# Token-major products read their moving columns in groups of four, odd groups first

## The chip, the cores and the metric

The kernel runs on one core of one Trainium2 chip. The metric is device time in microseconds for one execution of the whole program. The kernel before takes 3138.79 us (median of 3 runs, 3138.43 to 3139.48).

## The reference

Two transformer-like blocks over 256 tokens with 2048 features each, in float32. The first has a joint input projection, stick-breaking attention and chunked attention with relative bias, two sigmoid gates, an output projection, a gated feed-forward part with 5632 hidden features, and a gated addition from a second input. The second has a state-space branch, a gated linear attention branch, differential attention, three gates, an output projection, and a feed-forward part with a three-tap convolution over the tokens and 5504 hidden features. Cut to what matters here, every large step is a product of activations with a weight matrix that is read once:

```python
proj = h @ w_in[i]
merged = (jax.nn.sigmoid(gate_sb) * (y_sb @ w_sb_out[i])
          + jax.nn.sigmoid(gate_ca) * (y_ca @ w_ca_out[i]))
x = x + merged @ w_mix_out[i]
h = rmsnorm(x, g_ffn[i])
g_ff, u_ff = jnp.split(h @ w_ffn_in[i], 2, axis=-1)
x = x + (jax.nn.silu(g_ff) * u_ff) @ w_ffn_out[i]
```

With 256 tokens and some 580 MB of weights, the products are the work.

## The kernel before

**Precision.** A float32 product is made of three products in the format `fp32r`. Each factor is split into a high part (a cast to `fp32r`) and a low part (the rest): high x high, high x low and low x high are summed in PSUM. The split of the activations is kept in slots of 128 x 4 x 512, in which each feature tile has 256 high and 256 low columns. The split of the weights is made on the way: a DMA on the SP queue (line 476) brings half a megabyte, 128 x 1024, into a raw buffer; ACT casts it into the high ring (line 485, `high`), DVE subtracts for the low ring (line 495, `low`). Both rings lie in one tile `w`: five places of 1024 elements for the high parts, four for the low parts.

**Two kinds of products.** A *layer-major* job (`WS`) has the weights as the stationary operand and the tokens as the moving one: line 545 streams 512 columns (high and low tokens) through a high weight tile, line 549 streams 256 through a low one. The result has features on the partitions. A *token-major* job (`AS`) has the tokens as the stationary operand, 128 at a time, and the weights as the moving one: 512 weight columns stream through the tokens. The result has tokens on the partitions and 512 features along them. `mm_as` issues these: for each of the two feature tiles of a half and each of two token groups `m` there are three products, line 583 (low tokens, high weights), line 584 (high tokens, low weights) and line 585 (high, high). The very first half of the program takes another order, lines 573, 575 and 576. Each matmul instruction of the program carries its own weight load (LDWEIGHTS), which TensorE runs beside the matmul ahead of it.

**Order.** `stream` goes over all jobs in the order of the program and issues, half by half, the cast four halves ahead, the subtraction three halves ahead, the products of the half, and then lets the other generators (evacuation, attention, scans, norms) take one step. There is no scheduler behind it: each engine runs what was issued, in that order.

**Places.** When the halves of a layer-major job lie at the end of a ring turn, their places are shifted by `WSH` = 4 elements, 16 bytes (`places`, `far`). Token-major halves are never shifted.

**Layout.** The weights are laid out on the host before the timed run. `_as` makes the token-major layout: for each 512 columns, blocks of 256 rows as 128 partitions x 2 x 512. All token-major weights go through `_as` and are read by `mm_as` alone.

Of the kernel before, what the change touches and what calls it, by code (L numbers as in the profile page):

```python
# [53 lines left out]

def _as(w):

    K, N = w.shape
    if K % 256:
        w = np.concatenate([w, np.zeros((256 - K % 256, N), w.dtype)], axis=0)
        K = w.shape[0]  # L60
    return np.ascontiguousarray(
        w.reshape(K // 256, 2, 128, N // 512, 512).transpose(3, 0, 2, 1, 4).reshape(-1, 128, 1024))
# [12 lines left out]
def layout(x, p, w_in, w_sb_out, w_ca_out, w_mix_out, rel_bias, g_mix, g_ffn, g_ple, g_final, w_ffn_in,  # L75
# [35 lines left out]

    w = w_in[0]
    a["w_vsb"], a["w_vca"] = _as(w[:, 2048:3072]), _as(w[:, 5120:6144])
    a["w_qksb"] = _ws(w[:, 0:1024], w[:, 1024:2048])
    a["w_qkca"] = _ws(w[:, 3072:4096], w[:, 4096:5120])
    a["w_gsb"], a["w_gca"] = _as(w[:, 6144:8192]), _as(w[:, 8192:10240])
    a["w_sbo"], a["w_cao"], a["w_mix"] = _as(w_sb_out[0]), _as(w_ca_out[0]), _as(w_mix_out[0])
    a["w_fin"] = _ws(w_ffn_in[0][:, :5632], w_ffn_in[0][:, 5632:])
    a["w_fout"] = _as(w_ffn_out[0])
# [68 lines left out]
class Build:  # L188
# [373 lines left out]
    def mm_as(self, acts, ks, wh, wl, acc, ms, first, end, low_last=False):  # L562

        nc = self.nc
        if low_last:
            for low in (False, True):
                for kk, k in enumerate(ks):
                    s = slice(kk * 512, kk * 512 + 512)
                    for m in ms:
                        x = acts.at(k)  # L570
                        xh, xl = x[:, m * 128:m * 128 + 128], x[:, 256 + m * 128:384 + m * 128]
                        if low:
                            nc.tensor.matmul(acc[:, m, :], lhsT=xh, rhs=wl[:, s], start=False, stop=False)
                        else:
                            nc.tensor.matmul(acc[:, m, :], lhsT=xl, rhs=wh[:, s], start=k == first, stop=False)
                            nc.tensor.matmul(acc[:, m, :], lhsT=xh, rhs=wh[:, s], start=False, stop=False)
            return
        for kk, k in enumerate(ks):
            x = acts.at(k)
            s = slice(kk * 512, kk * 512 + 512)  # L580
            for m in ms:
                xh, xl = x[:, m * 128:m * 128 + 128], x[:, 256 + m * 128:384 + m * 128]
                nc.tensor.matmul(acc[:, m, :], lhsT=xl, rhs=wh[:, s], start=k == first, stop=False)  # L583
                nc.tensor.matmul(acc[:, m, :], lhsT=xh, rhs=wl[:, s], start=False, stop=False)  # L584
                nc.tensor.matmul(acc[:, m, :], lhsT=xh, rhs=wh[:, s], start=False, stop=k == end)  # L585


    def as_job(self, w, n, acts, evac, k0=0, nk=None, before=None, kt=None):
# [1205 lines left out]
```

## Time and profile before

| | before |
|---|---|
| median of 3 runs | 3138.79 us |
| profiled execution, whole | 3139.36 us |
| its span, first to last instruction | 3137.6 us |
| mean granted TensorE clock | 0.999 |
| TensorE busy | 3119.9 us, 99% |
| weight loads busy | 2651.4 us, 85% |
| DVE busy | 1993.1 us, 64% |
| ACT busy | 1553.3 us, 50% |
| moved by DMA | 618.00 MB, mean 197 GB/s |

PE is TensorE's matmuls, PEld its weight loads, DVE the vector engine, ACT the scalar engine. A row of a group gives the line, the engine, the operation, output and inputs with their shapes, the number of instructions, then the busy time in us (overlaps counted once), the mean duration of one in ns, and the idle time ahead of them with what ended it. A matmul's duration holds its way through the array, and the next one starts before it ends; the ends are modelled. A timeline row gives the start in us from the first instruction and the duration in us.

### The profile page before, as it was taken

What the parts mean: (1) busy time and instruction counts of PE and PEld (TensorE: products, weight loads), DVE (VectorE), ACT (ScalarE), POOL (GpSimd) and SP (SyncE); (2) the same over time, 40 slices, a digit from 0 to 9 for tenths busy, and PEclk for the clock granted to TensorE, in tenths of its full rate; (3) what the DMA queues carried; (4) which work ended last, traced back from release to release, by engine and by line L of the source; (5) the groups of instructions that cost most, each with busy time, mean ns of one, the idle gap of its engine ahead of it and who ended that gap; (6) DMA issues with size and microseconds to landing.
All of it is one profiled execution on the core that took longest, in us unless ns stands there. A gap on an engine that the chain in (4) does not pass through costs nothing.

```text
span 3137.6 us, 45166 instructions
## 1 busy us (share of the span) xinstructions
PE 3119.9 (99%) x17629; PEld 2651.4 (85%) x17629; DVE 1993.1 (64%) x2593; ACT 1553.3 (50%) x2035; POOL 73.4 (2%) x158
## 2 busy tenths in 40 slices
PE   9999999999999999999999999999999999999998
PEld 7888888888888888888888888888888888888887
DVE  5656445557577677566655667945555766757766
ACT  6544444455444454456544454444445654545545
POOL 0000000000001000000000001000000000000000
PEclk9999999999999999999999999999999999999999
DMA  7554555555667766655654575655555555555554
GB/s 265 170 180 163 189 194 187 182 189 189 216 224 243 255 224 233 198 175 189 216 181 162 174 221 197 211 191 199 200 186 181 190 195 186 191 196 188 192 188 168
DMA packets 172645, 618.00 MB, mean 197 GB/s; under 512 B 23552, under 2 KB 23968, under 8 KB 169232
## 3 DMA queue, kind: packets, MB, share of 16 engines
q1 hardware_dynamic: 164992, 577.49, 55.4%
q0 software_dynamic: 7440, 37.64, 3.5%
q8 instruction: 138, 2.26, 0.3%
q14 instruction: 75, 0.61, 0.1%
HBM read 599.74 MB, written 14.25 MB: 196 GB/s over the span
## 4 chain that ended last, share of the span: by engine, by line
PE 99%; ACT 0%; DMA 0%; DVE 0%; DVEq 0%; issue 0%; SPq 0%; ACTq 0%
PE acc L545 29%; PE acc L583 17%; PE acc L584 17%; PE acc L585 17%; PE acc L549 15%; PE p L348 1%; PE p L1699 0%; PE p L1739 0%; PE p L1156 0%; PE p L930 0%; PE p L931 0%; PE p L932 0%; PE p L1152 0%; PE p L1742 0%; PE p L1133 0%; PE p L1733 0%
## 5 line engine op out<-in xcount | busy, mean ns | idle before, releaser
L495 DVE TENSOR_TENSOR w<-raw,w 128x1024 fp32r<-128x1024 f32 x1088 | 1320.2, 1220 | 644.2 <-PE acc L584 421.7
L485 ACT CAST w<-raw 128x1024 fp32r<-128x1024 f32 x1088 | 1138.4, 1049 | 1092.4 <-PE acc L585 637.3
L545 PE MATMUL acc<-s,w 128*128 128x512 f32 x3936 | 1369.5, 393 | 0.0
L549 PE MATMUL acc<-s,w 128*128 128x256 f32 x3936 | 1090.4, 282 | 0.0
L583 PE MATMUL acc<-w,s 128*128 128x512 f32 x2372 | 932.4, 393 | 0.8 <-DVE big L1376 0.8
L585 PE MATMUL acc<-w,s 128*128 128x512 f32 x2372 | 923.6, 389 | 0.0
L584 PE MATMUL acc<-w,s 128*128 128x512 f32 x2372 | 923.5, 389 | 0.0
L545 PEld LDWEIGHTS acc<-s,w 128*128 128x128 f32 x3936 | 733.4, 188 | 153.5
L549 PEld LDWEIGHTS acc<-s,w 128*128 128x128 f32 x3936 | 740.2, 188 | 10.4 <-issue 1.0
L583 PEld LDWEIGHTS acc<-w,s 128*128 128x128 f32 x2372 | 445.6, 188 | 93.8 <-issue 1.7
L585 PEld LDWEIGHTS acc<-w,s 128*128 128x128 f32 x2372 | 445.3, 188 | 93.5
L584 PEld LDWEIGHTS acc<-w,s 128*128 128x128 f32 x2372 | 445.7, 188 | 90.9 <-issue 0.5
L445 DVE TENSOR_TENSOR s<-acc,s 128x512 f32<-128x512 f32 (+1 forms) x120 | 82.7, 690 | 263.8 <-ACT s L444 263.7
L444 ACT COPY s<-acc 128x512 f32<-128x512 f32 (+1 forms) x120 | 70.1, 585 | 189.1 <-PE acc L545 186.9
L312 ACT ACTIVATE s<-s 128x256 f32<-128x256 f32 (+4 forms) x175 | 76.6, 443 | 105.1 <-DVE s L315 38.0
L315 DVE SCALAR_TENSOR_TENSOR s<-s,conv 128x256 f32<-128x256 f32 x172 | 79.4, 482 | 3.1
L447 DVE TENSOR_TENSOR s<-s,rb 128x512 f32<-128x512 f32 (+1 forms) x104 | 71.7, 689 | 3.5
L320 ACT CAST s<-s 128x256 fp32r<-128x256 f32 (+1 forms) x104 | 45.7, 443 | 30.1 <-DVE s L970 15.0
L1655 DVE TENSOR_TENSOR s<-s,s 128x1024 f32<-128x1024 f32 x48 | 58.5, 1220 | 0.0
L312 ACT ACTIVATE s<-s,conv 128x256 f32<-128x256 f32 x86 | 47.1, 595 | 22.0 <-DVE s L447 22.0
L321 DVE TENSOR_TENSOR s<-s,s 128x256 fp32r<-128x256 f32 (+1 forms) x104 | 47.6, 460 | 15.8 <-ACT s L320 15.8
L312 ACT ACTIVATE junk<-big 128x512 f32<-128x512 f32 x48 | 30.3, 632 | 50.7 <-DVE big L949 32.4
(265 smaller groups left out, 1007.7 us busy)
## 6 DMA issues: line engine op xcount, KB each, us to landing
raw<-in_w_fin SPq DMA_DIRECT2D x176, 512.0 KB, 4.3
raw<-in_w_up SPq DMA_DIRECT2D x172, 512.0 KB, 4.0
raw<-in_w_fout SPq DMA_DIRECT2D x88, 512.0 KB, 4.3
raw<-in_w_down SPq DMA_DIRECT2D x84, 512.0 KB, 4.2
raw<-in_w_qksb SPq DMA_DIRECT2D x32, 512.0 KB, 3.8
raw<-in_w_qkca SPq DMA_DIRECT2D x32, 512.0 KB, 3.5
raw<-in_w_gsb SPq DMA_DIRECT2D x32, 512.0 KB, 3.9
raw<-in_w_gca SPq DMA_DIRECT2D x32, 512.0 KB, 4.2
```

Source lines behind the costliest of these rows:

```text
L312: self.nc.scalar.activation(out, in_, func, scale=scale, **kw)
L315: self.nc.vector.scalar_tensor_tensor(out=out, in0=in0, scalar=scalar, in1=in1, op0=op0, op1=op1)
L444: nc.scalar.copy(out, acc[:, 0:n, 256:512])
L445: nc.vector.tensor_add(out, acc[:, 0:n, 0:256], out)
L447: nc.vector.tensor_mul(out, out, rb.tile[:, None, :].to_broadcast([128, n, 256]) if n > 1 else rb.tile[:, None, :])
L485: nc.scalar.copy(wh[:, :n], raws[i][:, :n])
L495: nc.vector.tensor_sub(wl[:, :n], r[:, :n], wh[:, :n].bitcast(F32))
L545: hi = lambda: nc.tensor.matmul(acc[:, f, :], lhsT=wh[:, s], rhs=x, start=k == first, stop=k == end)
L549: nc.tensor.matmul(acc[:, f, 256:512], lhsT=wl[:, s], rhs=x[:, 0:256], start=False, stop=False)
L583: nc.tensor.matmul(acc[:, m, :], lhsT=xl, rhs=wh[:, s], start=k == first, stop=False)
L584: nc.tensor.matmul(acc[:, m, :], lhsT=xh, rhs=wl[:, s], start=False, stop=False)
L585: nc.tensor.matmul(acc[:, m, :], lhsT=xh, rhs=wh[:, s], start=False, stop=k == end)
```

## The change

The columns of each 512-wide block of a token-major weight are permuted on the host. Taken in groups of four (16 bytes), the stored order is: group 0 of the first 256 columns, group 0 of the second 256, group 1 of the first, group 1 of the second, and so on. `mm_as` then reads the moving operand with a pattern of three levels: two passes, 64 groups each, four columns in each group. The first pass takes the first, third, fifth .. group, the second pass the others. The columns arrive at TensorE, and in PSUM, in their old order. The patterns of the stationary operand, of PSUM and of the weights' casts and subtractions stay as they are.

```diff
 def _as(w):
     K, N = w.shape
+    w = w.reshape(K, N // 512, 2, 64, 4).transpose(0, 1, 3, 2, 4).reshape(K, N)
     if K % 256:
...
     def mm_as(self, acts, ks, wh, wl, acc, ms, first, end, low_last=False):
         nc = self.nc
+        def cols(w, kk):
+            return w[:, kk * 512:kk * 512 + 512].rearrange("p (i h c) -> p h i c", h=2, c=4)
...
         for kk, k in enumerate(ks):
             x = acts.at(k)
-            s = slice(kk * 512, kk * 512 + 512)
             for m in ms:
                 xh, xl = x[:, m * 128:m * 128 + 128], x[:, 256 + m * 128:384 + m * 128]
-                nc.tensor.matmul(acc[:, m, :], lhsT=xl, rhs=wh[:, s], start=k == first, stop=False)
-                nc.tensor.matmul(acc[:, m, :], lhsT=xh, rhs=wl[:, s], start=False, stop=False)
-                nc.tensor.matmul(acc[:, m, :], lhsT=xh, rhs=wh[:, s], start=False, stop=k == end)
+                nc.tensor.matmul(acc[:, m, :], lhsT=xl, rhs=cols(wh, kk), start=k == first, stop=False)
+                nc.tensor.matmul(acc[:, m, :], lhsT=xh, rhs=cols(wl, kk), start=False, stop=False)
+                nc.tensor.matmul(acc[:, m, :], lhsT=xh, rhs=cols(wh, kk), start=False, stop=k == end)
```

The three products of the first half (`low_last`) are changed in the same way.

More of the change, by code (lines that the diff above doesn't have):

```diff
@@ L572, in mm_as @@
                         if low:
-                            nc.tensor.matmul(acc[:, m, :], lhsT=xh, rhs=wl[:, s], start=False, stop=False)
+                            nc.tensor.matmul(acc[:, m, :], lhsT=xh, rhs=cols(wl, kk), start=False, stop=False)
                         else:
-                            nc.tensor.matmul(acc[:, m, :], lhsT=xl, rhs=wh[:, s], start=k == first, stop=False)
-                            nc.tensor.matmul(acc[:, m, :], lhsT=xh, rhs=wh[:, s], start=False, stop=False)
+                            nc.tensor.matmul(acc[:, m, :], lhsT=xl, rhs=cols(wh, kk), start=k == first, stop=False)
+                            nc.tensor.matmul(acc[:, m, :], lhsT=xh, rhs=cols(wh, kk), start=False, stop=False)
             return
@@ L579, in mm_as @@
             x = acts.at(k)
-            s = slice(kk * 512, kk * 512 + 512)
             for m in ms:
                 xh, xl = x[:, m * 128:m * 128 + 128], x[:, 256 + m * 128:384 + m * 128]
-                nc.tensor.matmul(acc[:, m, :], lhsT=xl, rhs=wh[:, s], start=k == first, stop=False)
-                nc.tensor.matmul(acc[:, m, :], lhsT=xh, rhs=wl[:, s], start=False, stop=False)
-                nc.tensor.matmul(acc[:, m, :], lhsT=xh, rhs=wh[:, s], start=False, stop=k == end)
+                nc.tensor.matmul(acc[:, m, :], lhsT=xl, rhs=cols(wh, kk), start=k == first, stop=False)
+                nc.tensor.matmul(acc[:, m, :], lhsT=xh, rhs=cols(wl, kk), start=False, stop=False)
+                nc.tensor.matmul(acc[:, m, :], lhsT=xh, rhs=cols(wh, kk), start=False, stop=k == end)
     def as_job(self, w, n, acts, evac, k0=0, nk=None, before=None, kt=None):
```

## The prediction

> **What bounds the kernel now.** I read the profile page first (busy shares, the chain that ended last, the costliest groups), then the timeline of one long stretch of token-major products, then three places where the same product runs under other conditions. The page:
>
> ```profile
> span 3137.6 us, 45166 instructions
> ...
> PE 3119.9 (99%) x17629; PEld 2651.4 (85%) x17629; DVE 1993.1 (64%) x2593; ACT 1553.3 (50%) x2035; POOL 73.4 (2%) x158
> ...
> PEclk9999999999999999999999999999999999999999
> ...
> PE 99%; ACT 0%; DMA 0%; DVE 0%; DVEq 0%; issue 0%; SPq 0%; ACTq 0%
> PE acc L545 29%; PE acc L583 17%; PE acc L584 17%; PE acc L585 17%; PE acc L549 15%; PE p L348 1%; PE p L1699 0%; PE p L1739 0%; PE p L1156 0%; PE p L930 0%; PE p L931 0%; PE p L932 0%; PE p L1152 0%; PE p L1742 0%; PE p L1133 0%; PE p L1733 0%
> ...
> L545 PE MATMUL acc<-s,w 128*128 128x512 f32 x3936 | 1369.5, 393 | 0.0
> L549 PE MATMUL acc<-s,w 128*128 128x256 f32 x3936 | 1090.4, 282 | 0.0
> L583 PE MATMUL acc<-w,s 128*128 128x512 f32 x2372 | 932.4, 393 | 0.8 <-DVE big L1376 0.8
> L585 PE MATMUL acc<-w,s 128*128 128x512 f32 x2372 | 923.6, 389 | 0.0
> L584 PE MATMUL acc<-w,s 128*128 128x512 f32 x2372 | 923.5, 389 | 0.0
> ```
>
> TensorE is busy for 99% of the span, the chain is TensorE from end to end, and the products show no idle time ahead of them. The token-major products are lines 583, 584 and 585, 51% of the chain. Whatever one of them gains or loses is gained or lost by the whole kernel, unless a supplier falls behind.
>
> The durations 389 and 393 ns overlap, because a product drains while the next one streams. What counts is the distance between starts, and that stands in the timeline (start, duration, engine, line):
>
> ```profile
> 999.82 0.39 PE L583 MATMUL acc<-w,s 128*128 128x512 f32 x1
> 999.82 0.19 PEld L584 LDWEIGHTS acc<-w,s 128*128 128x128 f32 x1
> 1000.04 0.39 PE L584 MATMUL acc<-w,s 128*128 128x512 f32 x1
> 1000.04 0.19 PEld L585 LDWEIGHTS acc<-w,s 128*128 128x128 f32 x1
> 1000.27 0.39 PE L585 MATMUL acc<-w,s 128*128 128x512 f32 x1
> ...
> 1005.93 0.39 PE L583 MATMUL acc<-w,s 128*128 128x512 f32 x1
> ```
>
> From the first row to the last are 27 products with nothing between: (1005.93 - 999.82) / 27 = 226.3 ns each. The weight load of the next product starts together with the product ahead of it and takes 0.19 us, so it is over before that product hands on. It costs something only if it disturbs the stream of moving columns.
>
> **The change, part by part.** The built program has the same instructions in the same order on every engine. They differ in one thing: the moving operand of 7128 matmuls (2372 x 3 on lines 583 to 585, and the 12 of the first half at lines 573 to 576) was one run of 512 elements, and is now two passes of 64 groups of four elements, each group 32 bytes after the last. The permutation of the weights that makes this right is done on the host, ahead of the timed run. No instruction, DMA, wait or byte is added; the casts (L485) and subtractions (L495) go over the same 1024 elements in a row. So the sum has one term: 7128 times the change in the 226.3 ns. A microsecond of the total is 0.14 ns of one product, and the 0.2% that a measurement of this kernel can tell from no change (6.3 us) is 0.9 ns.
>
> No matmul in the trace of before has a moving operand with gaps, so this term is bounded from both sides.
>
> What could be gained? Two rows give a floor. The first products of the kernel start at half the pace:
>
> ```profile
> 8.72 0.63 PE L575 MATMUL acc<-w,s 128*128 128x512 f32 x1
> ...
> 11.28 0.63 PE L573 MATMUL acc<-w,s 128*128 128x512 f32 x1
> ```
>
> Six starts in 2.56 us are 427 ns. The granted clock reads full there too, so what holds them back is not shown; if the array runs at exactly half its later pace, the full pace is 213.5 ns, and today's 226.3 has 12.8 ns too much: 7128 x 12.8 = 91 us, the most that a better order could bring (3048 us). A nearer floor is the page's pair L545 and L549: 256 more columns last 393 - 282 = 111 ns longer, so 512 columns stream in 222 ns and the excess is 4.3 ns, or 31 us (3109 us). That the two differ says that most of the 12.8 ns is a fixed cost per product, which the order of columns inside it would not touch.
>
> Is the excess a collision with the weight load, as an order by 16-byte groups would suggest? Line 585 is sometimes followed by a product on another tile of the array, whose weight load begins late:
>
> ```profile
> 1878.67 0.39 PE L585 MATMUL acc<-w,s 128*128 128x512 f32 x1
> ...
> 1878.98 0.33 PEld L1699 LDWEIGHTS p<-s,s 128*32 128x32 f32 x20 [0.35 <-issue]
> ```
>
> and the groups of lines in that instant (busy us, mean ns):
>
> ```profile
> L584 PE MATMUL acc<-w,s 128*128 128x512 f32 x1 | 0.4, 389 | 0.0
> L585 PE MATMUL acc<-w,s 128*128 128x512 f32 x1 | 0.4, 388 | 0.0
> ```
>
> Here no weight load runs beside the product (it starts 0.31 us after it), and the product lasts 388 ns, against 389 for its neighbour L584 with a load beside it. The ends are modelled, so this is a hint and no proof, but by it the ordinary weight load costs 1 ns, that is 7 us in all, and not 12.8. A second hint is the line at which a layer-major job follows. There the weights lie shifted by 16 bytes (WSH = 4 elements), so a load on line 545 reads its groups out of step with the moving operand of line 585, which is not shifted:
>
> ```profile
> 54.32 0.39 PE L585 MATMUL acc<-w,s 128*128 128x512 f32 x1
> 54.54 0.39 PE L545 MATMUL acc<-s,w 128*128 128x512 f32 x1
> ```
>
> The distance is 0.22 us, as with unshifted weights. The relative place of 16-byte groups does not show in the pace.
>
> The Trainium skill ("SBUF — State Buffer", the note on cachelines in the section on Door 1) says that lines are 16 bytes and that an access runs at full rate if it hits a line at least twice. By that rule four float32 fill a line in either order, 128 lines are read either way, and the sum would be zero; no run here shows a strided moving operand. Its section "Who interferes with whom" gives TensorE separate read ports for moving operand and weights, which would leave nothing to gain; against it stand the timeline and the mean duration at one place:
>
> ```profile
> 596.94 0.39 PE L585 MATMUL acc<-w,s 128*128 128x512 f32 x1
> 596.94 0.59 PEld L348 LDWEIGHTS p<-cst,big 128*128 128x128 f32 x4
> ```
>
> ```profile
> L585 PE MATMUL acc<-w,s 128*128 128x512 f32 x1 | 0.4, 393 | 0.0
> ```
>
> Beside the denser loads of a transpose the same product takes 393 ns instead of 389. So a weight load can hold up the stream, by 4 ns here.
>
> What could be lost? By this row, 4 ns for each product: 7128 x 4 = 29 us. If the excess of today came a second time, 12.8 ns: 91 us. And if the stream fell to the pace of the first products, 427 - 226.3 = 200.7 ns: 1431 us, 4570 us in all. Between these ends I take zero for the likeliest: groups stay whole, as many are read, and the order of groups relative to the weight load has left no mark in two places.
>
> The sum is made against the profiled execution: 3137.6 of span and 1.8 around it, 3139.4, plus 7128 x 0. It stands 0.6 above the median of the runs, 3138.8, so the forecast for the median is **3139 us**, with its own range from 3132 to 3146 (1 ns of weight load, 7 us, saved or doubled).
>
> A faster TensorE would not soon wait for its suppliers. In a stretch of mostly token-major work:
>
> ```profile
> 985.00:1061.00 76.00, 76.00 (x352) 63.46 (x351) 51.42 (x49) 31.56 (x34) 5.79 (x10) 1.00 0.71 235
> ```
>
> (columns: TensorE, weight loads, DVE, ACT, POOL busy with counts, granted clock, DMA share, GB/s) the DVE is busy for 51.4 of 76 us and the DMA engines for 71%. Even the full 12.8 of 226.3 ns (6%) leaves both below the bound. If that cover were gone, the waiting time would fall on TensorE one for one.
>
> **The rivals.**
>
> Slower by collisions. In the first pass the moving stream stays on every other group for 256 columns, about half of the product's time, and the next weight load runs in just that time. If memory is split by 16-byte groups into two halves, every second group of the load meets a half that is never free; today the two streams change halves all the time. For it speaks the 393 ns row; against it the shifted weights and the 388 ns row. Price: from 4 to 12.8 ns, 3168 to 3230, with the middle at 8.4 ns: 60 us, 3199. It decides from 0.9 ns on.
>
> Slower by the stream itself. If TensorE fetches more than 16 bytes at a time and throws away what the pass skips, or if two reads of one half cannot follow each other as quickly, the stream drops towards the half pace: up to 4570 us. Against it: nothing in the trace, since nothing like it ran; for it: 222 ns for 512 columns looks like a read path with little slack.
>
> Faster. The excess does come from the alternation of groups, and the grouped order takes part of it away: from 0.9 up to the 12.8 ns, 3133 down to 3048, with the nearer floor of 4.3 ns at 3109. For it: the 12.8 ns has no other name. Against it: the 388 ns row, where it stays with no load beside it, and the pair L545 and L549, where it does not grow with the columns. By the Trainium skill ("TensorE: Matmul & The Clock Gate", "Back-to-back issue gap") a warm product takes N / 2.4 + 2.5 ns, 215.8 for 512; an estimate by that page is a gain of at most 10.5 ns, 75 us; the trace stands at 226.3 and does not say whether a float32 product can reach it.
>
> That the change does nothing at all (the groups merged again into one run by the build) I leave out: the built matmuls carry the grouped pattern.
>
> **How the numbers follow.** No change 45%, slower by collisions 22%, slower by the stream 11%, faster 22%. So faster by over 0.2% is 0.22, within 0.2% 0.45, slower 0.33. The predicted time is that of the likeliest, 3139. Both signs hold more than half of the chance, so the range goes beyond 3132 to 3146: down to 3080, past the nearer floor and leaving out the larger part of the far one (some 6%), and up to 3235, past the collisions at 12.8 ns, leaving out the slower stream (11%) and little else.
>
> **What would show it.** Right: lines 583 to 585 keep 389 ns and 226 to 227 ns from start to start, and all other lines are as before. Collisions: these lines last 393 to 402 ns, and the same line with no load beside it stays at 388. A slower stream: far over 400 ns, with or without a load. Faster: 376 to 387 ns, with starts 214 to 225 ns apart, and then the waits of L583 for L485 and L495 have to be looked at, because the suppliers have less time. Wrong in kind would be any change in lines 545 and 549, since nothing of theirs was touched.

## The result, and the profile after

The changed kernel takes 3180.44 us (median of 3 runs, 3180.43 to 3181.26), before 3138.79. The ratio is 1.0133, with a 95% interval from 1.0119 to 1.0147: 41.7 us slower. The forecast was no change, 3139, in a range from 3080 to 3235. The time lies in the range, on the side of the rivals "slower"; it lies outside the 3132 to 3146 that the prediction gave to the value it took.

The page after (span, busy shares, chain, costliest groups; the lines have moved: 545 and 549 are now 547 and 551, and 583 to 585 are 588 to 590):

```profile
span 3178.7 us, 45166 instructions
...
PE 3160.9 (99%) x17629; PEld 2652.2 (83%) x17629; DVE 1993.5 (63%) x2593; ACT 1551.1 (49%) x2035; POOL 72.8 (2%) x158
...
PEclk9999999999999999999999999999999999999999
...
L547 PE MATMUL acc<-s,w 128*128 128x512 f32 x3936 | 1369.6, 393 | 0.0
L551 PE MATMUL acc<-s,w 128*128 128x256 f32 x3936 | 1090.5, 282 | 0.0
L588 PE MATMUL acc<-w,s 128*128 128x512 f32 x2372 | 945.7, 399 | 0.8 <-DVE big L1381 0.8
L589 PE MATMUL acc<-w,s 128*128 128x512 f32 x2372 | 937.7, 395 | 0.0
L590 PE MATMUL acc<-w,s 128*128 128x512 f32 x2372 | 936.9, 395 | 0.0
```

The granted clock and the layer-major lines are as before. TensorE is still busy for 99%, and the wait ahead of the products has not grown. The loss is in the three token-major lines alone, each some 6 ns longer. The timeline of a long stretch after the change (start, duration, engine, line) gives the distance between starts:

```profile
1016.19 0.40 PE L588 MATMUL acc<-w,s 128*128 128x512 f32 x1
1016.43 0.40 PE L589 MATMUL acc<-w,s 128*128 128x512 f32 x1
1016.66 0.40 PE L590 MATMUL acc<-w,s 128*128 128x512 f32 x1
...
1022.49 0.40 PE L588 MATMUL acc<-w,s 128*128 128x512 f32 x1
```

27 products in 6.30 us are 233.3 ns each; before, a like stretch gave 226.3. Over the some 6960 token-major products that are followed by another without a stall, the trace has 227.0 ns before and 233.0 after. 5.9 ns x 7128 = 42 us: the whole loss is the pace of the stream.

One row of the trace was named ahead as a sign: the product with no weight load beside it. The timeline, and the groups at that instant:

```profile
2062.82 0.39 PE L590 MATMUL acc<-w,s 128*128 128x512 f32 x1
...
2063.15 0.26 PEld L1736 LDWEIGHTS p<-xb,s 128*32 128x32 f32 x15 [0.37 <-issue]
```

```profile
L590 PE MATMUL acc<-w,s 128*128 128x512 f32 x1 | 0.4, 394 | 0.0
```

It lasts 394 ns, against 388 before. Each trace has 26 such places: after the change this line lasts 391 to 396 ns there, 394 on the mean, and before 388 in each. A collision with a load that stands beside the product cannot be the whole story, because here there is none.

### The profile page after: what moved, and what is told of

Read it like the earlier page. It is cut to its first block, busy times and chain, and to the rows that moved or that the text cites. A ratio compares the mean times of both kernels' runs of the same rounds, so it can differ in the third digit from the quotient of the medians.

```text
span 3178.7 us, 45166 instructions
## 1 busy us (share of the span) xinstructions
PE 3160.9 (99%) x17629; PEld 2652.2 (83%) x17629; DVE 1993.5 (63%) x2593; ACT 1551.1 (49%) x2035; POOL 72.8 (2%) x158
## 4 chain that ended last, share of the span: by engine, by line
PE 99%; ACT 0%; DMA 0%; DVE 0%; DVEq 0%; issue 0%; SPq 0%; ACTq 0%
PE acc L547 28%; PE acc L588 17%; PE acc L589 17%; PE acc L590 17%; PE acc L551 15%; PE p L350 1%; PE p L1704 0%; PE p L1744 0%; PE p L1161 0%; PE p L935 0%; PE p L937 0%; PE p L936 0%; PE p L1157 0%; PE p L1747 0%; PE p L1138 0%; PE p L1738 0%
## 5 line engine op out<-in xcount | busy, mean ns | idle before, releaser
L588 PE MATMUL acc<-w,s 128*128 128x512 f32 x2372 | 945.7, 399 | 0.8 <-DVE big L1381 0.8
L589 PE MATMUL acc<-w,s 128*128 128x512 f32 x2372 | 937.7, 395 | 0.0
L590 PE MATMUL acc<-w,s 128*128 128x512 f32 x2372 | 936.9, 395 | 0.0
```

Of the source, the lines that this page charges most:

```text
L588: nc.tensor.matmul(acc[:, m, :], lhsT=xl, rhs=cols(wh, kk), start=k == first, stop=False)
L589: nc.tensor.matmul(acc[:, m, :], lhsT=xh, rhs=cols(wl, kk), start=False, stop=False)
L590: nc.tensor.matmul(acc[:, m, :], lhsT=xh, rhs=cols(wh, kk), start=False, stop=k == end)
```

## The experiments

Theories at the start. *Levels*: a pattern of several levels costs a fixed amount. *Skips*: each step to a group that does not follow costs. *Halves*: memory is split by 16-byte lines into two halves (or four parts), and staying on one of them costs, in the stream itself or against the weight load. Each run below is compared with the kernel before on the same chip. In the first six, the host's permutation follows the pattern, so the work is the same.

### Other group sizes and distances

The edits are the two numbers of the pattern, `h` passes over groups of `c` columns (`H` and `C` below stand for them):

```diff
-            return w[:, kk * 512:kk * 512 + 512].rearrange("p (i h c) -> p h i c", h=2, c=4)
+            return w[:, kk * 512:kk * 512 + 512].rearrange("p (i h c) -> p h i c", h=H, c=C)
```

`h=2, c=8`:

> As the change, but groups of eight columns (32 bytes): two passes of 32 groups. The change cost 41.7 us, 5.8 ns for each of 7128 products. If each step to a group that does not follow costs (127 steps in the change, 63 here), 2.9 ns: 21 us over before, 3159. If any pattern of more than one level costs a fixed amount, the same 41.7: 3180. If memory is split by 16-byte lines into two halves and the stream is slowed by staying on one of them, a 32-byte group alternates again: no cost, 3139.

`h=2, c=128`:

> Groups of 128 columns, first, third, second, fourth: still three levels, but only three steps to a group that does not follow. Fixed cost of a pattern with levels: 3180. Cost per step (3 of 127): 0.1 ns a product, 3140. Cost of staying on one half of the 16-byte lines: none, 3139.

`h=4, c=4`:

> Groups of four columns in four passes, each group 64 bytes after the last. Cost per step: as the change, 3180. Fixed cost: 3180. Cost of staying on one half of the 16-byte lines: 3180, or more if there are four parts and not two (then the stream stays on one of four, and twice as many repeats or more: 3200 and above). If the weight load's collisions are what costs, the length of the pass over one part matters (107 ns in the change, 57 here, against a load that reads for about 107): a different time, by the halves theory the same.

`h=2, c=2`:

> Groups of two columns (8 bytes), two passes: each 16-byte line is visited twice, 256 visits a product in place of 128, and consecutive visits go to lines that follow each other, so the two halves alternate. Cost per step (255 in place of 127): 11.7 ns, 3222. Fixed cost: 3180. Cost of staying on one half: none, 3139; the rule that two hits on a line are enough says the same. If a visit to a line costs a fetch whatever is taken from it and fetches are the limit, far more: the stream at half pace, 4570.

`h=8, c=4`:

> Groups of four columns in eight passes, each group 128 bytes after the last. The four-pass order (64 bytes apart) took 3129.4, the two-pass order of the change (32 bytes apart) 3180.4. If the distance between consecutive lines is what counts, and only 32 bytes is bad, this is at 3125 to 3140. If four parts by 16-byte lines are in play, the stream stays on one of them here as with four passes: 3129. If more passes were the cost, it would be above 3139.

`h=2, c=16`:

> Groups of 16 columns (64 bytes), two passes, each group 128 bytes after the last. Groups of 4 and 8 columns in two passes cost 41.3 and 38.4 us, groups of 128 nothing. If cost follows the lines read from one half or quarter of a 64-byte block, whole 64-byte blocks are read here: 3139. If it falls off with the number of skips (31 here), about 10 us: 3149. If the cost lies in passing over memory twice while the weight load runs, it stays near 3177.

Measured (the pace is the mean distance of starts over all token-major products of the trace without a stall; "alone" is the mean duration of line 590 where no weight load runs beside it):

| passes x columns in a group | bytes from group to group | time, us | ratio to before, 95% interval | pace, ns | alone, ns |
|---|---|---|---|---|---|
| in order (before) | - | 3138.8 | - | 227.0 | 388 |
| 2 x 4 (the change) | 32 | 3180.4 | 1.0133 (1.0119 to 1.0147) | 233.0 | 394 |
| 2 x 8 | 64 | 3177.5 | 1.0122 (1.0109 to 1.0136) | 232.5 | 392 |
| 2 x 128 | 1024 | 3139.3 | 1.0001 (0.9992 to 1.001) | 227.0 | 388 |
| 4 x 4 | 64 | 3129.4 | 0.9969 (0.9957 to 0.9982) | 225.7 | 389 |
| 2 x 2 | 16 | 4736.5 | 1.5088 (1.5068 to 1.5109) | 451.9 | 633 |
| 8 x 4 | 128 | 3277.8 | 1.0443 (1.0429 to 1.0457) | 246.6 | 412 |
| 2 x 16 | 128 | 3230.7 | 1.0293 (1.0279 to 1.0307) | 240.0 | 404 |

What falls. *Levels*: groups of 128 columns have the three levels too and cost nothing. *Skips*: the order 4 x 4 has as many skips as the change and is faster than before; 2 x 16 has a quarter of them and costs twice as much. *Halves* of 16-byte lines: 4 x 4 stays on one half (or on one of four parts) in every pass and gains, while 2 x 8 and 2 x 16 change halves all the time and lose. No single count of lines, halves or skips puts these eight rows in order, and for 4 x 4, 8 x 4 and 2 x 16 no value that was expected came near the measured one.

What stands. Groups of two columns visit each 16-byte line twice, 256 visits a product instead of 128. The three lines of that run, from its page:

```profile
L588 PE MATMUL acc<-w,s 128*128 128x512 f32 x2372 | 1506.5, 635 | 0.8 <-DVE big L1381 0.8
L589 PE MATMUL acc<-w,s 128*128 128x512 f32 x2372 | 1501.1, 633 | 0.0
L590 PE MATMUL acc<-w,s 128*128 128x512 f32 x2372 | 1500.8, 633 | 0.0
```

They run at half the pace: 451.9 / 256 = 1.765 ns for each visit, and before it is 227.0 / 128 = 1.773 ns. In this run the time follows the visits to lines, not the columns: twice the visits for the same 512 columns take twice the time. Visits are not all: the other orders have 128 of them too and take from 225.7 to 246.6 ns. And a cost of reading in runs of 8 bytes, whatever the line, would look the same here; no run tells the two apart.

The faster order is worth a look. The page of 4 x 4, and a piece of its timeline:

```profile
span 3127.0 us, 45166 instructions
...
L588 PE MATMUL acc<-w,s 128*128 128x512 f32 x2372 | 924.2, 390 | 0.8 <-DVE big L1381 0.8
L590 PE MATMUL acc<-w,s 128*128 128x512 f32 x2372 | 915.7, 386 | 0.0
L589 PE MATMUL acc<-w,s 128*128 128x512 f32 x2372 | 915.6, 386 | 0.0
```

```profile
1004.61 0.39 PE L589 MATMUL acc<-w,s 128*128 128x512 f32 x1
1004.83 0.39 PE L590 MATMUL acc<-w,s 128*128 128x512 f32 x1
1005.06 0.38 PE L588 MATMUL acc<-w,s 128*128 128x512 f32 x1
1005.28 0.38 PE L589 MATMUL acc<-w,s 128*128 128x512 f32 x1
1005.50 0.38 PE L590 MATMUL acc<-w,s 128*128 128x512 f32 x1
1005.72 0.39 PE L588 MATMUL acc<-w,s 128*128 128x512 f32 x1
1005.95 0.40 PE L589 MATMUL acc<-w,s 128*128 128x512 f32 x1
1006.19 0.39 PE L590 MATMUL acc<-w,s 128*128 128x512 f32 x1
```

The distances are 0.22 and 0.23 us, with one of 0.24 between. They repeat: in nanoseconds this stretch of the program runs 220, 221, 221, 234, 239, 225, 226, and from the start again, through all three lines. Seven is a multiple neither of the three lines nor of the two token groups, so this beat does not come from the line.

The beat of seven is not what makes 4 x 4 faster: its mean is 226.6 ns, the pace of before. The gain lies in other rows of products. Take as a row the token-major products with no other line between them; 44 rows have 36 products or more, and from the eleventh distance on each of them keeps one pace to its end (the two halves of a row agree within 0.6 ns). A stretch of a faster row of 4 x 4:

```profile
1949.89 0.39 PE L589 MATMUL acc<-w,s 128*128 128x512 f32 x1
...
1956.14 0.39 PE L590 MATMUL acc<-w,s 128*128 128x512 f32 x1
```

These are 28 products in 6.25 us, 223.2 ns each. Over the whole trace:

| order | rows | settled pace, ns |
|---|---|---|
| in order (before) | 44 | 226.7, even (227, 227, 226: a steady 226.67 in whole ns) |
| 2 x 4 (the change) | 35 | 233.3, even or within 2 ns |
| 2 x 4 (the change) | 9 | 231.1 (228, 232, 233, 229, 231, 234) |
| 4 x 4 | 30 | 226.7 (the beat of seven) |
| 4 x 4 | 14 | 223.4 (230, 224, 221, 218) |
| 2 x 8 | 38 | 232.4 |
| 2 x 8 | 6 | 233.3 |
| 8 x 4 | 44 | 246.7 |
| 2 x 16 | 44 | 240.0 |

So an order has one or two paces, and the same instructions in the same order can settle at either. What decides it in a row was not found. I take this for two streams that fall into step with each other, the moving columns and the loads; the next runs test that.

### Shorter weight loads

Edit to before (and in the same way to the change and to 8 x 4):

```diff
         for kk, k in enumerate(ks):
             x = acts.at(k)
+            n = 128 if k in (first, end) else 64
             for m in ms:
-                xh, xl = x[:, m * 128:m * 128 + 128], x[:, 256 + m * 128:384 + m * 128]
+                xh, xl = x[:, m * 128:m * 128 + n], x[:, 256 + m * 128:256 + m * 128 + n]
...
-                nc.tensor.matmul(acc[:, m, :], ...
+                nc.tensor.matmul(acc[:n, m, :], ...
```

> Columns in order as before, but in all token-major products except those of a job's first and last feature tile the stationary operand has 64 token columns in place of 128, so that the weight load is half as long and the result of the second 64 tokens of each group is left out. The moving stream is the same 512 columns. If the 12.8 ns over 213.5 come from the weight load, 5 to 6 ns a product fall away: some 35 us less, 3105, plus a few us for changing the tile size twice a job. If they belong to the stream's own fetches, it stays: 3139 plus those few us.

> The order of the change with the half weight loads of the run beside it (the same results are left out). The comparison is with that run. If the cost of the change is collisions with the weight load, its 41 us halve to about 20. If the stream itself is slower in this order, the difference stays at some 35 to 41 us.

The same with 32 in place of 64:

> Columns in order, as before; in all token-major products except those of a job's first and last feature tile (1974 of 2372 on each line) the stationary operand has 32 token columns, so the weight load is a quarter as long, and the results of the other 96 tokens of each group are left out. Base for the two runs beside it. With half loads it was 3156.7, 18 us over before. If the 12.8 ns over 213.5 have nothing to do with the load, some 3140 to 3170; if the load causes them, three quarters of 12.8 ns go: 3080 or so.

> The order of the change (groups of four, two passes) with quarter weight loads; the same results are left out. Against the run in order beside it. If the order costs by meeting the reads of the weight load, the difference is a quarter of 41.7 or less on 83% of the products: 10 to 18 us. If the order makes the stream itself slower, 35 to 42 us. With half loads the difference was 11.4.

> Groups of four in eight passes, 128 bytes apart, with quarter weight loads; the same results are left out. With full loads this order cost 139 us. If by meeting the weight load: a quarter of it or less on 83% of the products, 25 to 60 us over the run in order beside it. If the stream itself is slower: 116 to 139 us over it.

Measured, with the pace of the products that have the shortened load on both sides:

| | full load | half | quarter |
|---|---|---|---|
| in order | 3138.8 us, 227.0 ns | 3156.7 us, 230.1 ns | 3168.3 us, 231.6 ns |
| 2 x 4 (the change) | 3180.4 us, 233.0 ns | 3168.1 us, 231.2 ns | 3166.0 us, 230.7 ns |
| 8 x 4 | 3277.8 us, 246.6 ns | not run | 3274.5 us, 246.4 ns |
| change less in order | 41.7 us | 11.4 us | -2.3 us |

Most of the expectations missed. The half load in order was put at 3105 or a few us over 3139; both differences between the orders lie below every value that was named; 8 x 4 with quarter loads is 106 us over the run in order, where 25 to 60 or 116 to 139 were named. Only the quarter load in order lies in a range (3140 to 3170), which was set after the half load was known.

The groups of the quarter run in order, from its grouped lines:

```profile
L589 PE MATMUL acc<-w,s 128*32 128x512 f32 x1974 | 784.2, 397 | 0.0
L591 PE MATMUL acc<-w,s 128*32 128x512 f32 x1974 | 777.6, 394 | 0.0
L590 PE MATMUL acc<-w,s 128*32 128x512 f32 x1974 | 777.5, 394 | 0.0
L589 PEld LDWEIGHTS acc<-w,s 128*32 128x32 f32 x1974 | 214.9, 109 | 227.7 <-issue 0.8
```

and its timeline, 24 products in 5.56 us, 231.7 ns each:

```profile
1008.19 0.40 PE L589 MATMUL acc<-w,s 128*32 128x512 f32 x1
...
1013.75 0.40 PE L589 MATMUL acc<-w,s 128*32 128x512 f32 x1
```

The loads are shorter (109 ns in place of 188) and the product in order is *longer*, 394 ns in place of 389. No mechanism named so far gives that: less work for the weight load costs 4.6 ns a product. And with quarter loads the change costs nothing more. By these runs the 41.7 us are not a price of the new order as such. They read as the loss of a good step that columns in order have with full loads (227.0 instead of 231.6), and 1.4 ns on top.

The trace of before points the same way without any edit. After a stall the products do not start at 226 ns; they take some time to settle (L583 at 161.81 waited, and the products after it):

```profile
162.13 0.39 PE L584 MATMUL acc<-w,s 128*128 128x512 f32 x1
162.35 0.39 PE L585 MATMUL acc<-w,s 128*128 128x512 f32 x1
162.58 0.40 PE L583 MATMUL acc<-w,s 128*128 128x512 f32 x1
162.82 0.39 PE L584 MATMUL acc<-w,s 128*128 128x512 f32 x1
163.05 0.40 PE L585 MATMUL acc<-w,s 128*128 128x512 f32 x1
163.28 0.39 PE L583 MATMUL acc<-w,s 128*128 128x512 f32 x1
163.51 0.39 PE L584 MATMUL acc<-w,s 128*128 128x512 f32 x1
163.74 0.39 PE L585 MATMUL acc<-w,s 128*128 128x512 f32 x1
163.96 0.39 PE L583 MATMUL acc<-w,s 128*128 128x512 f32 x1
164.19 0.39 PE L584 MATMUL acc<-w,s 128*128 128x512 f32 x1
164.42 0.39 PE L585 MATMUL acc<-w,s 128*128 128x512 f32 x1
```

From 162.13 to 163.51 are six products of 230 ns, from 163.51 to 164.42 four of 227.5. Over all such places of the trace, the first three distances after the stalled one are 232.1, 232.5 and 230.5 ns on the mean, the tenth and later ones 226.7. After the change the first three are 231.5, 233.4 and 232.1 and the later ones 233.0: the two orders start alike, and only columns in order settle to 226.7. The quarter run in order holds the other half of the comparison: it keeps full loads for a job's last and the next job's first feature tile, 12 products that follow one another, and from the ninth distance on these are back at 226.7 ns.

The order 8 x 4 behaves differently. With a quarter of the load it is as slow as with the full one (246.4 and 246.6 ns), and its product without a load lasts 412 ns. There the stream itself is slower, 15 ns above the 231.6 of columns in order, and these runs show no part of the load in it.

A caution: a load of 32 columns is also a narrower tile of the array. These runs cannot tell the length of the load from the width of the tile.

### More lines for the weight load

```diff
-                xh, xl = x[:, m * 128:m * 128 + 128], x[:, 256 + m * 128:384 + m * 128]
+                xh, xl = x[:, m:512:4], x[:, 2 + m:512:4]
```

> Moving columns in order, as before, full weight loads, but the stationary operand takes every fourth element of the 512 of a feature tile (tokens and high and low parts are mixed, so the results are other numbers; the work is the same). Each weight load then touches 128 lines of 16 bytes in place of 32. If reads of the load get in the way of the moving stream, each product becomes longer: at the fetch time of 1.77 ns a line that the run with groups of two showed, up to 96 x 1.77 = 170 ns, 1200 us in all; at the 6 ns of the change as the price of 32 lines, 18 ns more, 130 us. If the two do not meet, and a load of 128 fetches still fits beside a product (227 ns), 3139.

Measured: 3203.65 us, ratio 1.0206 (1.0192 to 1.022), pace 235.1 ns. The groups of its lines:

```profile
L584 PE MATMUL acc<-w,s 128*128 128x512 f32 x2372 | 944.0, 398 | 0.0
...
L584 PEld LDWEIGHTS acc<-w,s 128*128 128x128 f32 x2372 | 737.0, 311 | 0.3
```

The run is 65 us over before; 0, 130 and up to 1200 were named. The load lasts 311 ns in place of 188, longer than the 235 ns from product to product, and the idle time ahead of the loads of line 584 fell from 90.9 us to 0.3: the loads run back to back. The product may wait for its own load here, and need not be slowed by meeting it. This run does not tell the two apart. An estimate of what a line costs the load: with 128, 64 and 32 columns the loads of the runs above last 188, 135 and 109 ns, which is 83 ns and 0.82 ns for each column. Less the same 83 ns, the 128 lines here take 228 ns, 1.78 ns each, as much as a visit of the moving stream. The 311 ns may hold some waiting, so this is a hint and no proof.

## Why the prediction was right or wrong

**What bounds the kernel**: right. 5.9 ns a product over 7128 products gives 42 us, and 41.7 were measured; no other line moved, and no supplier came into play. That the time lies in the range is owed to the widening for the rivals, and as far as the mechanism goes it is luck: the one term of the sum was put at zero and came out at 5.9 ns.

**The value taken, zero**: wrong, and this is the step that failed. It rested on "the order of groups relative to the weight load has left no mark in two places". Both places were read in the wrong way. The 388 ns of a product without a load beside it was taken as the price of the load, 1 ns. But the pace is a property of a run of products that have settled; one product at its end says nothing of what sets the beat. The runs with shorter loads put a number on it: without the full load (or the full tile, which changed with it), columns in order run at 231.6 ns and not at 227. The shifted weights on line 545 were one product at the end of such a run as well.

**The excess of 12.8 ns as a fixed cost per product**: not borne out. Twice 213.5 ns and 12.8 would be 440; groups of two columns took 451.9, twice the time for twice the visits, 1.765 ns a visit against 1.773. So the excess grew with the visits in that run; orders with 128 visits differ by as much, so this is no proof. The nearer floor from the pair of layer-major lines, 4.3 ns, was no floor of the mechanism, though the one order that gained, 1.3 ns on the mean and 3.3 in its faster rows, stayed within it.

**The rival "slower by collisions"**, priced from 4 to 12.8 ns with 8.4 in the middle: the measured 5.9 ns lies in it, and it is true that order and weight load act together (41.7, 11.4, -2.3 us as the load shrinks). Its picture is not: there are no two halves by 16-byte lines on which staying costs (4 x 4), beside a full load columns in order run faster than beside a quarter load and not slower, and its sign, 388 ns for the product without a load, came out as 394. Nor does the load run in just the time of the first pass: its rows show 188 ns of the 226. What the runs point to is the loss of a favourable step, not of freedom from collisions.

The row of 393 ns that spoke for it was a single one. Of 21 products of line 585 that the trace of before has ahead of these transposes, 12 last 400 ns, 5 last 393 and 4 last 388, so denser loads there go with as much as 11 ns; the price taken from that row was low.

**The rival "slower by the stream itself"**: not seen in the change, since with quarter loads it is as fast as columns in order. But it exists: 8 x 4 loses 15 ns with any load, and groups of two fell to 4736 us, near the 4570 that was worked out for a stream at half pace.

**The rival "faster"**: came true in another order, not in this one. 4 x 4 takes 3129.4 us, 0.31% less than before (0.18% to 0.43%), and beats both kernels.

**The Trainium skill**: the rule on 16-byte lines ("SBUF — State Buffer", the note on cachelines) says that two hits on a line are enough for the full rate. The run with groups of two float32, two hits a visit, went at half the pace; four hits a visit, as in order, had the full one, and three were not run. Here the measurement decides. The 215.8 ns of "TensorE: Matmul & The Clock Gate" was reached by no order; single products of 4 x 4 came to 218.

**What stays open.** Why full loads and columns in order settle at 226.7 ns, why 32 bytes from group to group settle at 233.3 or 231.1, why 64 bytes in four passes settle at 223.4 in some rows and at 226.7 in others, and what makes the two orders with 128 bytes slow. The runs show that these are so; the structure behind them was not found. That the two streams that fall into step are the moving columns and the loads is the best reading of the half and quarter runs. It is argued and not shown, because the width of the tile changed too.

## What to carry to other kernels

Where TensorE is busy from end to end, read the distance between starts to the nanosecond over a long stretch and look at the first products after a stall as well: here the pace settled to a value of its own for each order, and a change of the access pattern alone, with 16 bytes or more in a group, moved the whole kernel by -0.3% to 4.4% without a wait showing anywhere. Look at single rows of products too, because one order can settle at two paces. Do not read the moving operand in runs of 8 bytes: for these 4-byte columns they cost half the speed. Try such orders in pairs of runs rather than reason them out: of six orders tried here beside the change, one gained 0.3%, one was even, and four lost from 1.2 to 51%.

## What the runs showed of the hardware that was not expected

- Twice the visits to 16-byte lines took twice the time: 128 visits in order 227.0 ns, 256 visits 451.9 ns, 1.77 ns each, for the same 512 columns of 4 bytes.
- A product beside a shorter weight load of a narrower tile can be slower: 227.0, 230.1 and 231.6 ns with stationary tiles of 128, 64 and 32 columns.
- Products in a long row settle to one pace and keep it: 226.7 ns in order, 233.3 or 231.1 in the change, 226.7 or 223.4 in 4 x 4. Some of these paces are even, others a beat that repeats after 4, 6 or 7 products.
- The two orders with 128 bytes from group to group were slower than those with 32 or 64: 246.6 ns for groups of 16 bytes, 240.0 ns for groups of 64. With 1024 bytes (groups of 512) it was 227.0.
- The activity of DVE and ACT leaves no mark on the pace: with both idle or both busy for most of a product, the mean distance after line 583 is 227.1 ns in both cases before, and 233.0 in both after the change (line 588; stalls left out). So the change did not lose its 42 us by meeting the casts and subtractions.
